# Three of the eight tiles of a depthwise convolution, computed in plain fp32 on 32x32 parts of the matmul array

## The chip, the cores and the metric

The kernel runs on one core of a Trainium2 chip. A core has a matmul engine (TensorE, PE in the profile; its weight loads are shown apart as PEld), a vector engine (DVE), a scalar engine (ACT), a general engine (POOL) and queues that issue DMA (SP and POOL here). The metric is the device time of one execution, in microseconds; shown is the median over runs.

## The reference, cut to what matters

The input is 512 positions of 1024 channels in fp32. There are two layers. The first has a state-space and attention mixer, the second a convolution module; each is followed by a layer norm, a square-relu MLP with 4096 hidden units, and another layer norm. The change lies in the convolution module of the second layer and in the addition that feeds its layer norms:

```python
def conformer_conv(x, w_pw1, b_pw1, w_dw, b_dw, ln_g, ln_b, w_pw2, b_pw2):
    h = x @ w_pw1 + b_pw1                       # 512 x 2048
    val, gate = jnp.split(h, 2, axis=-1)
    h = val * jax.nn.sigmoid(gate)              # 512 x 1024
    h = lax.conv_general_dilated(               # depthwise: 31 taps, each channel by itself
        h, w_dw[:, None, :], window_strides=(1,), padding=[(CONV_SIZE - 1, 0)],
        dimension_numbers=('NWC', 'WIO', 'NWC'), feature_group_count=CONV_WIDTH) + b_dw
    h = jax.nn.silu(layer_norm(h, ln_g, ln_b))
    return h @ w_pw2 + b_pw2

x = layer_norm(DEEPNORM_ALPHA * x + mix, ...)
x = layer_norm(DEEPNORM_ALPHA * x + sqrelu_mlp(x, ...), ...)
```

## The kernel before, in words

**Layout.** Activations are kept transposed: a tile is 128 channels by 512 positions, and 1024 channels are eight tiles (`KT`). A dense product is made in a split form: every fp32 operand is held as a high and a low half in a rounded fp32 format (fp32r), and each block of a product is three matmuls, high by high, high by low, low by high (`gemm`, whose matmuls carry L225). The weights of the conv module are split early in the program, kept in device memory, and fetched again by DMA from POOL's queue (L88).

**The convolution, tile by tile.** `glu_tile(j)` makes tile j's value `pv` and gate `pg` (24 matmuls each), takes a sigmoid on ACT (`csg`), multiplies on DVE (`hp`, fp32, with 30 zeros ahead for causality), and splits `hp` into `hph` (a cast on ACT, L215) and `hpl` (a subtraction on DVE, L216). The first two tiles' value and gate (`pl`) are made earlier, inside the layer norm ahead.

A depthwise tap scales each channel by its own weight. The kernel has two ways of doing it:
- `taps_pe`: ACT builds a 128x128 diagonal matrix with the tap's 128 weights, high part `dh` and low part `dl` (L154), and PE makes three matmuls with it into the accumulator `cv` (L1076). `DBUFS` is the number of buffers that these matrices rotate through.
- `taps_dve`: DVE makes one multiply-add over the tile for each tap (L357), in two running sums `cy` and `cz`. The first tap of each sum is made by ACT. At the end DVE adds `cy`, `cz` and `cv`.

`PE_TAPS` says how many of the 31 taps of each tile go to PE; the rest go to DVE, but for the two on ACT. The last two tiles (6 and 7) are worked in two halves of 256 positions: the first row of `PE_TAPS` holds for whole tiles and first halves, the second row for second halves. So PE makes 2+6+8+9+11+14 = 50 full-width taps and 13+14+13+8 = 48 half-width taps.

**What sets the order.** The code is written as a program, and the framework puts each engine's instructions into an order from the order in the program, the buffers and the data they need. Each engine then works through its own list in order. In the loop over the first six tiles, tile j+2's value and gate and tile j+1's PE taps are written ahead of tile j's DVE taps. `TAIL` is the written order for the halves of tiles 6 and 7: P for PE taps, V for DVE taps, G for the second half of the gate, N for the layer norm of one half. Then `tail_norm_lead` makes the second pointwise product (`tld`) and the next layer norm, with the first products of the MLP (`fl`) already begun. The two halves of that norm are reduced over channels by matmuls with a matrix of ones (L879: `mpc`, `vpc`), over sums `sc` that `LN.add` gathers tile by tile on DVE.

The matmul results rotate through PSUM: six banks of 128x512 fp32 for `pv`, `pg`, `cv` (`nps`), two for others (`stp`).

Of the kernel before, what the change touches and what calls it, by code (L numbers as in the profile page):

```python
# [9 lines left out]
F32 = mybir.dt.float32  # L10
# [155 lines left out]
def kernel(ctx: ExitStack, tc: tile.TileContext, a: dict, out: bass.AP):  # L166
# [47 lines left out]
    def split(hi, lo, src):  # L214
        i0 = S.copy(hi, src).ins  # L215
        i1 = V.tensor_sub(lo, src, hi.bitcast(F32)).ins  # L216
        return i0.name, i1.name
# [134 lines left out]
    def tt(o, x, y, op):  # L352
        V.tensor_tensor(o, x, y, op=op)  # L353
        return o
# [505 lines left out]
    class LN:  # L860
# [4 lines left out]

        def add(self, j, ys, c0, c1):

            if j == 1:
                self.s[c0] = tmp(f"s{self.n}{c0}")[:, c0:c1]
            if j:  # L870
                (V if j == KT - 1 or self.n in LN_ON_V else G).tensor_tensor(self.s[c0], ys[0][:, c0:c1] if j == 1 else self.s[c0], ys[j][:, c0:c1], op=ALU.add)

        def colmean(self, srcs, c0, c1, nm, other):

# [141 lines left out]
    wdh = hid.tile([P, KT, CONV], F32R, tag="wdh", name="wdh")  # L1016
    wdl = hid.tile([P, KT, CONV], F32, tag="wdl", name="wdl")

    def taps():
        for f in range(2):  # L1020
            wn = tmp(f"wn{f}")[:CONV]
            nc.sync.dma_start(wn, a["conv_w_dw"][0][:, f * T : (f + 1) * T])
            ps = stp(f"wd{f}")
            for i in range(4):
                PE.transpose(ps[:, i * 32 : i * 32 + CONV], wn[:, i * P : (i + 1) * P], ident[:CONV, :CONV])
            V.tensor_copy(wdw[:, 4 * f : 4 * f + 4, :], ps[:, :P].rearrange("p (i t) -> p i t", t=32)[:, :, :CONV])
        V.tensor_copy(wdh, wdw)
        V.tensor_sub(wdl, wdw, wdh.bitcast(F32))

    k0 = 0  # L1030
    for bi, nb in enumerate(FFN_BLOCKS[0]):
# [13 lines left out]
    def glu_tile(j, c0=0, c1=T):  # L1045
        if c0 == 0:
            if j < 2:
                ps[j] = first[2 * j : 2 * j + 2]
            else:
                ws[j], ps[j] = (W.next(), W.next()), (nps(f"pv{j}"), nps(f"pg{j}"))  # L1050
            hps[j] = hpage(f"hp{j}", F32, PAD + T), hpage(f"hph{j}", F32R, PAD + T), hpage(f"hpl{j}", F32R, PAD + T)
        vps, gps = ps[j]
        if j >= 2:
            gemm(vps, ws[j][0], slice(0, P), xs, c0, c1)
            gemm(gps, ws[j][1], slice(0, P), xs, c0, c1)
        sg = tmp(f"csg{j}{c0}")
        act(sg[:, c0:c1], gps[:, c0:c1], AF.Sigmoid, bias=pv("conv_b_pw1", 8 + j))
        hp, hh, hl = hps[j]
        p0 = PAD + c0 if c0 else 0
        if c0 == 0:  # L1060
            V.memset(hp[:, :PAD], 0.0)
        stt(hp[:, PAD + c0 : PAD + c1], vps[:, c0:c1], pv("conv_b_pw1", j), sg[:, c0:c1], ALU.add, ALU.mult)
        split(hh[:, p0 : PAD + c1], hl[:, p0 : PAD + c1], hp[:, p0 : PAD + c1])

    def taps_pe(j, c0=0, c1=T):
        _, hh, hl = hps[j]
        if c0 == 0:
            cps[j] = nps(f"cv{j}")
        n = PE_TAPS[c0 > 0][j]
# [5 lines left out]
            for i, (u, v) in enumerate(((dh, hh), (dh, hl), (dl, hh))):  # L1075
                PE.matmul(cps[j][:, c0:c1], u, v[:, t + c0 : t + c1], start=t == 0 and i == 0, stop=t == n - 1 and i == 2)  # L1076

    def taps_dve(j, c0=0, c1=T):

        hp = hps[j][0]  # L1080
        if c0 == 0:
            acc[j] = page(f"cy{j}", F32), hpage(f"cz{j}", F32)
        y, z = (x[:, c0:c1] for x in acc[j])
        t = CONV - 1
        act(y, hp[:, t + c0 : t + c1], AF.Identity, bias=pv("conv_b_dw", j), scale=wdw[:, j, t : t + 1])
        t = CONV - 2
        opened = act(z, hp[:, t + c0 : t + c1], AF.Copy, scale=wdw[:, j, t : t + 1])
# [3 lines left out]
        tt(y, y, z, ALU.add)  # L1091
        tt(y, y, cps[j][:, c0:c1], ALU.add)
        return opened

    ln = LN("c")
    n = KT - SPLIT_TILES
    cs_, ws, ps = None, [None] * KT, [None] * KT
    glu_tile(0)
    glu_tile(1)
    taps_pe(0)  # L1100
    for j in range(n):
        if j + 2 < KT:
            W.ahead = AHEAD[j + 2 >= n]
            glu_tile(j + 2, 0, T if j + 2 < n else H)
        if j + 1 < n:
            taps_pe(j + 1)
        opened = taps_dve(j)
        if j == 1:
            with tc.issue_after(opened):
                for i in range(KT):  # L1110
                    act(X[i], X[i], AF.Identity, bias=rb[2][:, i : i + 1], scale=ALPHA)
        for c0, c1 in HALVES:
            ln.add(j, [x and x[0] for x in acc], c0, c1)
    for o in TAIL:
        j, (c0, c1) = int(o[1]), HALVES[int(o[-1])]
        if o[0] == "P":
# [128 lines left out]
```

## Time and profile before

| What | Value |
|---|---|
| Time, median of 3 runs | 1219.02 us (1215.46 to 1219.36) |
| The profiled execution's own time | 1217.5 us |
| Its span in the trace | 1215.8 us |
| PE busy, share of the span | 1187.4 us, 98% |
| DVE busy | 786.9 us, 65% |
| ACT busy | 557.1 us, 46% |
| Mean clock granted to PE | 0.995 of full speed |

Times in the trace count from the span's start. The share of busy time is a mean over stages that differ, so a stage is read by a view that gives each engine's busy time in a stretch of the span. A PE matmul's end is modelled, so the time that a row of equal matmuls takes is read from start to start, or as the length of a stretch over their count. An fp32 matmul that is not in the fp32r format appears as two records.

### The profile page before, as it was taken

What the parts mean: (1) busy time and instruction counts of PE and PEld (TensorE: products, weight loads), DVE (VectorE), ACT (ScalarE), POOL (GpSimd) and SP (SyncE); (2) the same over time, 40 slices, a digit from 0 to 9 for tenths busy, and PEclk for the clock granted to TensorE, in tenths of its full rate; (3) what the DMA queues carried; (4) which work ended last, traced back from release to release, by engine and by line L of the source; (5) the groups of instructions that cost most, each with busy time, mean ns of one, the idle gap of its engine ahead of it and who ended that gap; (6) DMA issues with size and microseconds to landing.
All of it is one profiled execution on the core that took longest, in us unless ns stands there. A gap on an engine that the chain in (4) does not pass through costs nothing.

```text
span 1215.8 us, 16751 instructions
## 1 busy us (share of the span) xinstructions
PE 1187.4 (98%) x6546; PEld 1007.5 (83%) x6546; DVE 786.9 (65%) x1400; ACT 557.1 (46%) x990; POOL 58.2 (5%) x125
## 2 busy tenths in 40 slices
PE   9899999999999999999999999899999999999997
PEld 7677776789988888888999888889988888888885
DVE  7998774578745635646566999998843443434446
ACT  6836665734525524425323456964651332323230
POOL 1001101100000000000022110102000000000000
PEclk9999999999999999999999999999999999999999
DMA  8510042150878787887454631406142232323211
GB/s 205 155 49 22 19 130 61 31 195 1 264 250 282 251 284 264 270 283 268 165 183 159 213 104 36 139 1 208 39 152 87 87 108 83 122 70 121 70 52 69
DMA packets 128943, 168.86 MB, mean 139 GB/s; under 512 B 11298, under 2 KB 101666, under 8 KB 128864
## 3 DMA queue, kind: packets, MB, share of 16 engines
q1 hardware_dynamic: 120064, 136.30, 34.5%
q0 software_dynamic: 8640, 31.46, 7.6%
q8 instruction: 51, 0.84, 0.3%
q14 instruction: 28, 0.23, 0.1%
q10 hardware_dynamic: 160, 0.03, 0.0%
HBM read 132.12 MB, written 35.65 MB: 138 GB/s over the span
## 4 chain that ended last, share of the span: by engine, by line
PE 83%; DVE 10%; ACT 4%; DMA 2%; issue 1%; POOL 0%; SPq 0%; DVEq 0%; POOLq 0%; ACTq 0%
PE f L225 23%; PE g L1175 12%; PE acf L225 11%; PE fl L225 5%; PE tld L225 4%; PE tlb L225 4%; PE h L1159 3%; PE cv L1076 2%; PE pv L225 2%; PE pg L225 2%; PE tla L225 2%; PE pl L225 2%; DVE cz L357 1%; PE acmo L225 1%; PE av L709 1%
## 5 line engine op out<-in xcount | busy, mean ns | idle before, releaser
L102 DVE TENSOR_TENSOR wlo<-raw,whi 128x1024 fp32r<-128x1024 f32 x176 | 213.4, 1224 | 199.5 <-ACT whi L101 198.7
L101 ACT CAST whi<-raw 128x1024 fp32r<-128x1024 f32 x176 | 182.1, 1049 | 313.5 <-PE g L1175 107.4
L1175 PE MATMUL g<-whi,hh 128*128 128x512 f32 x208 | 81.8, 393 | 0.0
L1175 PE MATMUL g<-wlo,hh 128*128 128x512 f32 x208 | 81.8, 393 | 0.0
L1175 PE MATMUL g<-whi,hl 128*128 128x512 f32 x208 | 81.7, 393 | 0.0
L225 PE MATMUL f<-xah,whi 128*128 128x512 f32 x208 | 81.2, 390 | 0.0
L225 PE MATMUL f<-xdl,whi 128*128 128x512 f32 x208 | 81.1, 390 | 0.0
L225 PE MATMUL f<-xah,wlo 128*128 128x512 f32 x208 | 81.0, 390 | 0.0
L225 PE MATMUL f<-xdh,whi 128*128 128x512 f32 x208 | 81.0, 390 | 0.0
L225 PE MATMUL f<-xal,whi 128*128 128x512 f32 x208 | 81.0, 390 | 0.0
L225 PE MATMUL f<-xdh,wlo 128*128 128x512 f32 x208 | 81.0, 390 | 0.0
L225 PE MATMUL acf<-hl,whi 128*128 128x512 f32 x192 | 75.7, 394 | 0.0
L225 PE MATMUL acf<-hh,wlo 128*128 128x512 f32 x192 | 75.6, 394 | 0.0
L225 PE MATMUL acf<-hh,whi 128*128 128x512 f32 x192 | 75.5, 393 | 0.0
L215 ACT CAST hh<-fr 128x512 fp32r<-128x512 f32 x64 | 39.7, 621 | 59.6 <-DVE fr L353 59.6
L216 DVE TENSOR_TENSOR hl<-fr,hh 128x512 fp32r<-128x512 f32 x64 | 44.1, 690 | 31.9 <-ACT hh L215 31.8
L357 DVE SCALAR_TENSOR_TENSOR cy<-hp,wdw,cy 128x512 f32<-128x512 f32 (+1 forms) x99 | 63.6, 654 | 0.2
L357 DVE SCALAR_TENSOR_TENSOR cz<-hp,wdw,cz 128x512 f32<-128x512 f32 (+1 forms) x93 | 60.0, 656 | 0.0
L353 DVE TENSOR_TENSOR fr<-fr 128x512 f32<-128x512 f32 x64 | 43.7, 685 | 14.7 <-ACT fr L154 14.6
L1175 PEld LDWEIGHTS g<-wlo,hh 128*128 128x128 f32 x208 | 39.1, 188 | 8.9
L1175 PEld LDWEIGHTS g<-whi,hl 128*128 128x128 f32 x208 | 39.1, 188 | 8.9
L1175 PEld LDWEIGHTS g<-whi,hh 128*128 128x128 f32 x208 | 39.1, 188 | 8.8
(684 smaller groups left out, 3093.4 us busy)
## 6 DMA issues: line engine op xcount, KB each, us to landing
raw<-in_ffn_w_dram SPq DMA_DIRECT2D x48, 1024.0 KB, 5.8
raw<-in_ffn_w_dram SPq DMA_DIRECT2D x32, 512.0 KB, 3.5
kepth<-whi SPq DMA_DIRECT2D x30, 512.0 KB, 8.6
keptl<-wlo SPq DMA_DIRECT2D x30, 512.0 KB, 9.4
whi<-kepth POOLq DMA_DIRECT2D x30, 512.0 KB, 3.7
wlo<-keptl POOLq DMA_DIRECT2D x30, 512.0 KB, 4.5
raw<-in_conv_w_pw_dram SPq DMA_DIRECT2D x12, 1024.0 KB, 6.5
raw<-in_mix_w_in_dram SPq DMA_DIRECT2D x16, 512.0 KB, 3.9
```

What stands on the lines that cost most here:

```text
L101: i0 = nc.scalar.copy(hi, raw).ins
L102: i1 = nc.vector.tensor_sub(lo, raw, hi.bitcast(F32)).ins
L215: i0 = S.copy(hi, src).ins
L216: i1 = V.tensor_sub(lo, src, hi.bitcast(F32)).ins
L225: ins = PE.matmul(ps[:, c0:c1], u[:, k, ksl], v[:, c0:c1], start=start and k == 0 and i == 0, stop=stop and k == n - 1 and i == 2).ins
L353: V.tensor_tensor(o, x, y, op=op)
L357: V.scalar_tensor_tensor(o, x, s, y, op0=op0, op1=op1)
L709: ins = PE.matmul(av[R, P * kb :], vt[:, kb, R], ws_[f"{c}{h}"][0][:, o : o + T - P * kb], start=summed[h] == 1, stop=summed[h] == 4, skip ...
L1076: PE.matmul(cps[j][:, c0:c1], u, v[:, t + c0 : t + c1], start=t == 0 and i == 0, stop=t == n - 1 and i == 2)
L1159: PE.matmul(ps, u, v, start=k == 0 and i == 0, stop=k == nk - 1 and i == 2)
L1175: PE.matmul(pss[b], u, v[:, kk, :], start=k + kk == 0 and i == 0, stop=k + kk == nb - 1 and i == 2)
```

## The change

1. Tiles 2, 4 and 5 (`ON_PE`) have all 31 taps on PE, in plain fp32, by `taps_32`. The array is used as 16 parts of 32x32. Row part g works on channels 32g to 32g+31; the weights of tap t go to column part t modulo 4. One DVE operation builds the weights `D`: 31 blocks of 128x32, each a stack of four 32x32 diagonals. Each of the 31 taps then takes four matmuls (one per row part), 124 in all, each over 512 positions, into four PSUM banks `cw` (bank g for row part g). Within a bank, partitions 32c to 32c+31 hold the sum over the taps with t modulo 4 equal to c.
2. `merge` adds the four column parts: ACT copies each of the four banks to SBUF (`cq`), and one fp32 matmul each, with a stack of four identities (`mask`, 128x32), sums them into partitions 32g to 32g+31 of bank `cn`. `biased` moves that to SBUF with the bias, on ACT. These three tiles have no `hph`, `hpl`, no diagonals and no taps on DVE.
3. `PE_TAPS`: tiles 0 and 1 have all taps on DVE and ACT, tile 3 has 7 on PE, tile 6's halves 8 and 5, tile 7's 10 and 13. So the old form on PE falls to 7 full-width and 36 half-width taps.
4. `DBUFS` falls from 6 to 3. A tile's DVE taps are cut into three parts (`PARTS`), and a string `CONV_ORDER` gives the order: g for value and gate, p and m for the old and new PE taps, o for the merge, v for a third of the DVE taps, f for the bias of a merged tile, x for the scaling of the residual. `TAIL` begins with tile 7's first half.
5. `LN.add` starts its running sum with the first tile that is ready instead of with tile 0. The engine that does it is the same as before, DVE.

The order that the framework makes of it, at three places. First PE, after tile 2's value and gate (`pv`, `pg`), before:

```order
L225 MATMUL pg_6310<-xbh_5707,wlo_6252 128x512
L1076 MATMUL cv_6368<-hph_6266,dh_6369 128x512 [waits Activation_49]
L1076 MATMUL cv_6368<-hpl_6267,dh_6369 128x512 [waits DVE_49]
L1076 MATMUL cv_6368<-hph_6266,dl_6370 128x512
L1076 MATMUL cv_6368<-hph_6266,dh_6376 128x512
```

`hph_6266` is tile 1's: 18 such matmuls follow the gate of tile 2, on data that were made one tile earlier. And now, at the same place:

```order
L228 MATMUL pg_6299<-xbl_5712,whi_6255 128x512
L228 MATMUL pg_6299<-xbh_5711,wlo_6256 128x512
L1086 MATMUL cw_6378<-hp_6300,D_6376 32x512 [waits DVE_49]
L1086 MATMUL cw_6379<-hp_6300,D_6376 32x512
L1086 MATMUL cw_6380<-hp_6300,D_6376 32x512 [waits Activation_49]
L1086 MATMUL cw_6381<-hp_6300,D_6376 32x512
```

The matmuls after tile 2's gate now read `hp_6300`, which is tile 2's own and is made on DVE from that very gate. Second, PE at the end of the 124 matmuls, where the merge stands (now):

```order
L1086 MATMUL cw_6381<-hp_6300,D_6376 32x512
L228 MATMUL pv_6546<-xbh_5697,whi_6278 128x512 [waits DMASW4_49,Activation_49]
L228 MATMUL pv_6546<-xbl_5698,whi_6278 128x512
L228 MATMUL pv_6546<-xbh_5697,wlo_6279 128x512 [waits DMASW5_49]
L1095 MATMUL cn_6517<-cq_6518,mask 32x512 [waits Activation_49]
L1095 MATMUL cn_6517<-cq_6521,mask 32x512 [waits Activation_49]
L228 MATMUL pv_6546<-xbh_5699,whi_6278 128x512
L1095 MATMUL cn_6517<-cq_6524,mask 32x512 [waits Activation_49]
L228 MATMUL pv_6546<-xbl_5700,whi_6278 128x512
L228 MATMUL pv_6546<-xbh_5699,wlo_6279 128x512
L1095 MATMUL cn_6517<-cq_6527,mask 32x512 [waits Activation_49]
L228 MATMUL pv_6546<-xbh_5701,whi_6278 128x512
```

`pv_6546` is tile 3's value. The four merging matmuls stand among its matmuls in three places, each behind an ACT copy. The same pattern stands behind tile 4's 124 matmuls, in the value of tile 5. Behind tile 5's, six value matmuls of tile 6, three merging ones, four of tile 7 and the last merging one follow. Third, DVE, around the time when `hp` of tile 2 is made (now):

```order
L360 SCALAR_TENSOR_TENSOR cy_6353<-hp_6259,wdw,cy_6353 128x512 [waits DVE_49]
L360 SCALAR_TENSOR_TENSOR cz_6354<-hp_6259,wdw,cz_6354 128x512 [waits DVE_49]
L360 SCALAR_TENSOR_TENSOR hp_6300<-pv_6298,PV,csg_6349 128x512 [waits Activation_49]
L360 SCALAR_TENSOR_TENSOR cz_6354<-hp_6259,wdw,cz_6354 128x512 [waits DVE_49]
L360 SCALAR_TENSOR_TENSOR cy_6353<-hp_6259,wdw,cy_6353 128x512
```

`hp_6300` stands inside tile 0's chain of taps. `D_6376`, tile 2's weights, is built long before the convolution; `D_6747`, tile 4's, uses the same single buffer and stands later on DVE, waiting for the last of tile 2's 124 matmuls.

The diff, without the row of `LN.add` and of the tap loading that only follow from it:

```diff
-PE_TAPS = ((2, 6, 8, 9, 11, 14, 13, 14), (10, 10, 10, 10, 10, 10, 13, 8))
-TAIL = "P60 P70 V60 V70 G61 G71 N0 P71 P61 V61 V71 N1".split()
-DBUFS = 6
+PE_TAPS = ((0, 0, 0, 7, 0, 0, 8, 10), (10, 10, 10, 10, 10, 10, 5, 13))
+TAIL = "P70 P60 V60 V70 G61 G71 N0 P71 P61 V61 V71 N1".split()
+DBUFS = 3
+ON_PE = (2, 4, 5)
+PARTS = 3
+CONV_ORDER = "g0 g1 p0 g2 v0 p1 v0 m2 v0 o2 x0 g3 v1 f2 v1 g4 p3 m4 v3 v1 o4 g5 g6 m5 v3 o5 f4 v3 f5 g7".split()
...
-            hps[j] = hpage(f"hp{j}", F32, PAD + T), hpage(f"hph{j}", F32R, PAD + T), hpage(f"hpl{j}", F32R, PAD + T)
+            hps[j] = hpage(f"hp{j}", F32, PAD + T), *(() if j in ON_PE else (hpage(f"hp{x}{j}", F32R, PAD + T) for x in "hl"))
...
-        split(hh[:, p0 : PAD + c1], hl[:, p0 : PAD + c1], hp[:, p0 : PAD + c1])
+        if j not in ON_PE:
+            split(*(x[:, p0 : PAD + c1] for x in hps[j][1:] + (hp,)))
+
+    def taps_32(j):
+
+        D = hid.tile([P, CONV, 32], F32, tag="D", name=f"D{j}", bufs=1)
+        V.tensor_tensor(D, mask.unsqueeze(1).broadcast_to([P, CONV, 32]), wdw[:, j, :].unsqueeze(2).broadcast_to([P, CONV, 32]), op=ALU.mult)
+        cps[j] = [nps(f"cw{j}{g}") for g in range(4)]
+        for t in range(CONV):
+            for g in range(4):
+                R, C = slice(32 * g, 32 * g + 32), slice(32 * (t % 4), 32 * (t % 4) + 32)
+                PE.matmul(cps[j][g][C, :], D[R, t, :], hps[j][0][R, t : t + T], start=t < 4, stop=t >= CONV - 4,
+                          tile_position=(32 * g, 32 * (t % 4)))
+
+    def merge(j):
+
+        ps_ = stp(f"cn{j}")
+        for g in range(4):
+            q = tmp(f"cq{j}{g}")
+            S.copy(q, cps[j][g])
+            PE.matmul(ps_[32 * g : 32 * g + 32, :], mask, q, start=True, stop=True, tile_position=(0, 32 * g))
+        cps[j] = ps_
+
+    def biased(j):
+        acc[j] = page(f"cy{j}", F32), None
+        act(acc[j][0], cps[j], AF.Identity, bias=pv("conv_b_dw", j))
...
-        for i, t in enumerate(range(CONV - 3, PE_TAPS[c0 > 0][j] - 1, -1)):
+        n = PE_TAPS[c0 > 0][j]
+        todo = list(enumerate(range(CONV - 3, n - 1, -1)))
+        for i, t in todo[len(todo) * part // parts : len(todo) * (part + 1) // parts]:
...
-    for j in range(n):
...
+    for o in CONV_ORDER:
+        k, j = o[0], int(o[1])
+        if k == "g":
+            W.ahead = AHEAD[j >= n]
+            glu_tile(j, 0, T if j < n else H)
...
+        elif k != "p" or PE_TAPS[0][j]:
+            {"p": taps_pe, "m": taps_32, "o": merge}[k](j)
```

More of the change, by code (lines that the diff above doesn't have):

```diff
@@ L866, in add @@
         def add(self, j, ys, c0, c1):
[L868 to L871, printed above, removed]
+            y = ys[j][:, c0:c1]
+            if c0 not in self.s:
+                self.s[c0] = y
+            else:
+                if (c0, 0) not in self.s:
+                    self.s[c0, 0] = tmp(f"s{self.n}{c0}")[:, c0:c1]
+                tt(self.s[c0, 0], self.s[c0], y, ALU.add)
+                self.s[c0] = self.s[c0, 0]
         def colmean(self, srcs, c0, c1, nm, other):
@@ L1015 @@
     wdw = hid.tile([P, KT, CONV], F32, tag="wdw", name="wdw")
-    wdh = hid.tile([P, KT, CONV], F32R, tag="wdh", name="wdh")
-    wdl = hid.tile([P, KT, CONV], F32, tag="wdl", name="wdl")
+    most = max(PE_TAPS[0] + PE_TAPS[1])
+    wdh = hid.tile([P, KT, most], F32R, tag="wdh", name="wdh")
+    wdl = hid.tile([P, KT, most], F32, tag="wdl", name="wdl")
+    mask = hid.tile([P, 32], F32, tag="mask", name="mask")
     def taps():
@@ L1026, in taps @@
             V.tensor_copy(wdw[:, 4 * f : 4 * f + 4, :], ps[:, :P].rearrange("p (i t) -> p i t", t=32)[:, :, :CONV])
-        V.tensor_copy(wdh, wdw)
-        V.tensor_sub(wdl, wdw, wdh.bitcast(F32))
+        V.tensor_copy(wdh, wdw[:, :, :most])
+        V.tensor_sub(wdl, wdw[:, :, :most], wdh.bitcast(F32))
+        tt(mask, ident[:, :32], ident[:, 32:64], ALU.add)
+        tt(mask, mask, ident[:, 64:96], ALU.add)
+        tt(mask, mask, ident[:, 96:], ALU.add)
     k0 = 0
@@ L1057, in glu_tile @@
         act(sg[:, c0:c1], gps[:, c0:c1], AF.Sigmoid, bias=pv("conv_b_pw1", 8 + j))
-        hp, hh, hl = hps[j]
+        hp = hps[j][0]
         p0 = PAD + c0 if c0 else 0
@@ L1089, in taps_dve @@
             o = (y, z)[i % 2]
             stt(o, hp[:, t + c0 : t + c1], wdw[:, j, t : t + 1], o, ALU.mult, ALU.add)
-        tt(y, y, z, ALU.add)
-        tt(y, y, cps[j][:, c0:c1], ALU.add)
-        return opened
+        if part == parts - 1:
+            tt(y, y, z, ALU.add)
+            if n:
+                tt(y, y, cps[j][:, c0:c1], ALU.add)
     ln = LN("c")
     n = KT - SPLIT_TILES
[L1097 to L1100, printed above, removed]
-    for j in range(n):
[L1102 to L1109, printed above, removed]
+    cs_, ws, ps, last = None, [None] * KT, [None] * KT, {}
@@ L1110 @@
+    part = [0] * KT
+    for o in CONV_ORDER:
[3 more added lines that the diff above has]
+            glu_tile(j, 0, T if j < n else H)
+        elif k == "x":
+            with tc.issue_after(last["opened"]):
                 for i in range(KT):
                     act(X[i], X[i], AF.Identity, bias=rb[2][:, i : i + 1], scale=ALPHA)
-        for c0, c1 in HALVES:
-            ln.add(j, [x and x[0] for x in acc], c0, c1)
+        elif k in "vf":
+            if k == "f":
+                biased(j)
+            else:
+                part[j] += 1
+                taps_dve(j, 0, T, part[j] - 1, PARTS)
+                if part[j] < PARTS:
+                    continue
+            for c0, c1 in HALVES:
+                ln.add(j, [x and x[0] for x in acc], c0, c1)
+        elif k != "p" or PE_TAPS[0][j]:
+            {"p": taps_pe, "m": taps_32, "o": merge}[k](j)
```

15 lines of the change are left out of this document (8 added, 7 removed).

## The prediction, made before the changed kernel was timed

> **What bounds the kernel now.** I read the page first, then each stage of the convolution by engine, then the chain of waits.
>
> ```profile
> span 1215.8 us, 16751 instructions
> PE 1187.4 (98%) x6546; PEld 1007.5 (83%) x6546; DVE 786.9 (65%) x1400; ACT 557.1 (46%) x990; POOL 58.2 (5%) x125
> PE 83%; DVE 10%; ACT 4%; DMA 2%; issue 1%; POOL 0%; SPq 0%; DVEq 0%; POOLq 0%; ACTq 0%
> 628.00:667.07 39.07, 38.93 (x309) 38.15 (x308) 27.18 (x66) 14.45 (x30) 8.45 (x16) 1.00 0.56 189
> 667.07:757.13 90.06, 90.06 (x441) 75.83 (x440) 89.05 (x145) 50.11 (x131) 9.53 (x18) 1.00 0.37 126
> 757.13:778.76 21.63, 21.63 (x179) 21.32 (x177) 21.63 (x49) 19.20 (x61) 3.17 (x6) 1.00 0.36 118
> 778.76:795.48 16.72, 10.49 (x54) 9.03 (x55) 16.32 (x46) 14.88 (x39) 1.06 (x2) 0.90 0.29 100
> 795.48:848.70 53.22, 53.19 (x423) 52.36 (x424) 48.19 (x132) 29.29 (x71) 6.37 (x12) 1.00 0.35 118
> ```
>
> The lower rows are stretches of the span; behind the length stand the busy times of PE, PEld, DVE, ACT and POOL, then PE's granted clock. The changed code lies in 667 to 795 us. PE is busy in all of it but the fourth stretch, so time moves nearly one for one with PE's work there. DVE is as full as PE: 89.05 of 90.06 us in the second stretch. The one hole is 16.72 - 10.49 = 6.2 us in the fourth stretch, with a lower clock:
>
> ```profile
> PEld cv L1076 <- ACT hph L215: 4.2, 1, 4.2
> PEld cv L1076 <- ACT dh L154: 1.5, 1, 1.5
> 782.81 0.39 PE L1076 MATMUL cv<-hph,dh 128*128 128x256 f32 x1 [4.05 <-ACT hph L215]
> 783.96:789.03 5.07, 4.13 (x22) 3.86 (x23) 0.00 (x0) 0.74 0.01 2
> ```
>
> PE sits 4.05 us before the first tap of a second half; `hph` is late because its source `hp` stands on DVE behind a chain of taps. In the 5.07 us after it the clock is 0.74, which costs 0.26 x 5.07 = 1.3 us. Hole and clock together are about 7.5 us.
>
> **What is removed from PE.** Rows for the old matmuls (the first is from the chain: start, length, count; the second is a stretch of matmuls of 256 columns):
>
> ```profile
> 728.31 7.67 PE cv L1076 x33
> 629.68:641.28 11.60, 11.60 (x96) 11.53 (x96) 1.36 (x3) 1.00 0.94 313
> ```
>
> One full-width matmul takes 7.67/33 = 0.232 us, a half-width one 11.60/96 = 0.121 us. Full-width taps fall from 50 to 7: 43 x 3 x 0.232 = 29.9 us. Half-width ones fall from 48 to 36: 12 x 3 x 0.121 = 4.4 us. Removed: 34.3 us.
>
> **What is added on PE: the 124 matmuls.** The trace has no matmul on a 32x32 part. The nearest rows are plain fp32, whole array and column strips of 32:
>
> ```profile
> 650.50 1.74 PE vpb L879 x8
> 78.70:80.35 1.65, 1.64 (x62) 1.45 (x62) 0.00 (x0) 1.00 0.05 10
> 78.71 1.72 PE L528 MATMUL tp<-Cx,Gx 128*32 128x128 f32 x62
> 80.35 0.49 PE L542 MATMUL vI<-U,gt 128*128 128x128 f32 x2
> ```
>
> A plain fp32 record of 256 columns takes 1.74/8 = 0.2175 us, so one of 512 takes 0.435, and a product, which is two records, 0.87. The `tp` matmuls use strips of 32 columns of the array. 62 records of 128 columns end within 1.65 us. In one strip, 15.5 records of 128 columns would take 15.5 x 0.435/4 = 1.69 us by themselves, so the four strips run at the same time. It also bounds the issue from above: a record with its weight load needs no more than 1.65/62 = 27 ns. For row parts there are two rows of heads that use 64 rows each:
>
> ```profile
> 218.05 0.34 PE L672 MATMUL z3B<-ql,kh 64*128 64x384 f32 x1
> 218.23 0.33 PE L672 MATMUL z3B<-qh,kl 64*128 64x384 f32 x1
> 218.23 0.44 PE L672 MATMUL z3B<-qh,kh 64*128 64x384 f32 x2
> 218.46 0.38 PE L672 MATMUL z3B<-ql,kh 64*128 64x128 f32 x2
> ```
>
> A matmul of the second head (lower row half) starts in the same instant, 218.23, as one of the first head. So two row parts do run at once, and so do four column parts; that four by four do, no row shows. If all 16 run at once, the longest column part has 8 taps, and each row part takes its own: 8 x 0.87 = 7.0 us for a tile. The issue of 248 records takes 248 x 27 ns = 6.7 us at most, just under that. With a start of some 0.3 us, and a change of the array's partition at both ends, for which
>
> ```profile
> PEld vR L540 <- issue: 0.8, 4, 0.2
> ```
>
> gives 0.2 us (the switch from strips to the whole array), a tile costs 7.0 + 0.3 + 0.2 = 7.5 us. Lower bound 6.9 (nothing beside the matmuls), upper bound serial work, taken up under the rivals. I take 7.5, as the `tp` row has the same weights and the same strips. Three tiles: 22.5 us.
>
> **The merges.** Four plain fp32 matmuls of 0.87 us, each on its own strip of 32 columns, each behind an ACT copy of a bank. The nearest copy and the ACT and DVE steps that matter below:
>
> ```profile
> L1151 ACT COPY X<-xt 128x512 f32<-128x512 f32 x8 | 4.1, 620 | 0.0
> L160 ACT ACTIVATE csg<-pg,PV 128x512 f32<-128x512 f32 x4 | 2.7, 684 | 24.9 <-PE pg L225 24.9
> L357 DVE SCALAR_TENSOR_TENSOR hp<-pl,PV,csg x2: 747/750/752, 662.8 to 668.8; 128x512 f32<-128x512 f32 x2
> L357 DVE SCALAR_TENSOR_TENSOR cy<-hp,wdw,cy 128x512 f32<-128x512 f32 x64 | 46.5, 746 | 0.2
> L102 DVE TENSOR_TENSOR wlo<-raw,whi 128x1024 fp32r<-128x1024 f32 x176 | 213.4, 1224 | 199.5 <-ACT whi L101 198.7
> ```
>
> In PE's order a merge has three places: two products, one, one. The first two overlap, so three turns of 0.87 = 2.6 us; three visits to the strips with 0.2 us for the way in and out make 0.6. Three value matmuls stand ahead of the first, 0.7 us, and the first copy needs 0.62 and a signal: a wait of about 0.4 in all. That is 3.6 us a merge, 10.8 for three. From below: all four products at once, and one visit, 0.87 + 0.2 = 1.1 a merge, 3.2 in all; not likely, since the order has full-array matmuls between them. From above: each copy waited for alone, 4 x (0.62 + 0.87) + 6 x 0.2 = 7.2 a merge, 21.5 in all.
>
> **Waits that are added and removed.** The first of tile 2's 124 now reads tile 2's own `hp`. Behind the last `pg` come the sigmoid (0.68), then up to one tap of 0.66 that DVE is in, then `hp` (0.75), which PE must sit through: 0.68 + 0.75 + half a tap, and signals, about 1.9 us; bounds 1.4 and 2.3. Queued behind it on PE is the value of tile 3, for which nobody waits at that moment, but PE is the bound, so it counts. Tile 4's has the 21 old tap matmuls of tile 3 between (21 x 0.232 = 4.9 us) and tile 5's the half gate of tile 6 (48 x 0.121 = 5.8 us), so these two waits are covered. `D` (like the 128x1024 row, 1.2 us) is built by DVE well ahead.
>
> ```profile
> 757.38 0.66 DVE cy L357
> L357 DVE SCALAR_TENSOR_TENSOR cy<-hp,wdw,cy 128x256 f32<-128x256 f32 x35 | 17.1, 488 | 0.0
> 667.92 0.39 ACT L154 ACTIVATE dh<-ident,wdh 128x128 fp32r<-128x128 f32 x1
> 668.21 0.39 ACT L154 ACTIVATE dl<-ident,wdl 128x128 fp32r<-128x128 f32 x1
> 668.50 0.39 ACT L154 ACTIVATE dh<-ident,wdh 128x128 fp32r<-128x128 f32 x1
> ```
>
> DVE loses 124 - 80 = 44 full taps at 0.66 us (its step in the chain), gains 80 - 68 = 12 half ones at 0.49, three builds of `D`, and loses three subtractions for `hpl`: about 21 us less. ACT loses 55 pairs of diagonals and gets 12 copies and three bias moves. That takes pressure off `hp` of the second halves. It does not take the taps away that stand ahead of it: the halves have more DVE taps than before, 80 for 68. I let a third of the 7.5 us go, 2.5 us; bounds 0 and 7.5. `DBUFS` of 3 I cost at nothing: 15 or 18 half taps stand together instead of 21, ACT makes a pair in about 0.6 us (from 667.92 to 668.50) against 0.36 us of PE for a half tap, so ACT is behind within a run whatever the depth, and deeper buffers only store a lead of three pairs, at most 3 x 0.6 = 1.8 us for a run; that is inside the bounds of this term. `LN.add` moves no engine's work.
>
> **The sum**: -34.3 + 22.5 + 10.8 + 1.9 - 2.5 = -1.6 us. Against the profiled execution (span 1215.8, own time 1217.5) that is 1215.9; the median of the runs shown is 1.5 above that execution, so the prediction is 1217.4 us. The own range of this case: merges 2.5 less or 5 more for all three, the wait term between 0 and 5, together 1213 to 1222. What a measurement of this kernel can tell from no change is about 0.3%, 3.7 us, so "the same" is 1215.4 to 1222.7.
>
> [...] The rows `tp` and `z3B` show records that run beside each other. [...]
>
> **Rivals.**
>
> 1. *More is gained.* With DVE 21 us lighter the second halves' `hp` comes in time, and the hole and the slow clock after it go altogether: 5.0 us beyond the 2.5. For it: the hole is the only stretch in which PE idles, and it is DVE's queue that makes it. Against it: the half taps on DVE grow. -1.6 - 5.0 = -6.6, that is 1212.4.
>
> 2. *Fewer row parts at once (the side of slower).* The rows show two row parts at once, not four, and none where row and column parts are both cut. If two of the four run at a time, the 124 matmuls take 14.0 us instead of 7.0: 3 x 7.0 = +21.0 us, and the sum is +19.4: 1238.4. It decides from where the sum passes +3.7 us, 5.3 us above mine: when a tile's 124 take over 7.5 + 5.3/3 = 9.3 us. For it: no row speaks for four. Against it: nothing in the `z3B` rows shows two as a limit.
>
> 3. *Strict order.* Each product's second record waits for its first: 124 x 0.435 = 54 us a tile instead of 7.0, +141 us in three: 1358. Speaking against it: `tp`, where the same order would have cost 62 x 0.109 = 6.8 us and took 1.65.
>
> 4. *The merges cost their upper bound.* Copies are waited for one by one, since only three and one full-array matmuls (0.7 and 0.23 us) cover a copy of 0.62: 21.5 instead of 10.8, the sum is +9.1: 1228. For it: these covers are thin. Against it: ACT can make all four copies in a row.
>
> **Chances.** My forecast 0.50, more gained 0.20, fewer row parts 0.15, dear merges 0.10, strict order 0.05. Faster by over 0.3% (below 1215.4): 0.15 of the forecast's half and 0.18 of the first rival, 0.33. Within: 0.32, and 0.02 each of the first and the fourth, 0.36. Slower: 0.03, 0.08, 0.15 and 0.05, 0.31. The range is 1209 to 1240: it leaves out strict order, the upper part of the second rival and the lowest of the first.
>
> **What would show it.** In the changed profile the `cw` group: 248 records in about 7.0 us for a tile, from its first start to the next `pv`; 14 us would show two row parts, 54 strict order. The three `cn` visits of a merge: 3.6 us beyond the value matmuls between them. An idle entry of about 1.9 us before the first `cw`, put down to DVE's `hp`, and none before those of tiles 4 and 5. The stretch of the old hole: an idle time before a second half's first `cv` of 2 to 4 us, with a clock below 1. In the removed part, `cv` groups of 21 and 108 records at the same 0.232 and 0.121 us. The prediction fails if the overlap is partial, or if DVE, not PE, sets the end of the convolution.

## The result, and the profile after

The changed kernel takes 1221.86 us (median of 10 runs), the kernel before 1217.65 us (median of 10). The ratio is 1.0028, 95% interval 1.0017 to 1.0040: about 3.4 us slower (2.1 to 4.9 by the interval; the two medians lie 4.2 apart), where 1.6 us faster was forecast. The time lies inside the range that was given, but on the other side of the kernel before. The profiled execution has a span of 1219.3 us, 3.5 us more than the one before.

The page of the changed kernel, its first two rows:

```profile
span 1219.3 us, 17760 instructions
PE 1192.0 (98%) x7149; PEld 996.0 (82%) x7149; DVE 761.8 (62%) x1363; ACT 526.2 (43%) x886; POOL 58.2 (5%) x125
```

DVE has lost 25 us and ACT 31, and PE has 5 us more to do. The stretches of the convolution (length, then busy time of PE, PEld, DVE, ACT, POOL, then PE's clock):

```profile
679.56:718.86 39.30, 39.30 (x373) 27.27 (x374) 34.61 (x56) 10.70 (x24) 4.21 (x8) 1.00 0.40 132
718.86:748.12 29.26, 29.26 (x353) 20.19 (x353) 17.80 (x30) 4.06 (x8) 2.11 (x4) 1.00 0.22 73
748.12:768.10 19.98, 19.98 (x324) 13.73 (x323) 6.90 (x17) 5.01 (x11) 0.00 (x0) 1.00 0.01 2
768.10:784.01 15.91, 15.85 (x132) 15.83 (x132) 15.85 (x41) 13.65 (x44) 3.16 (x6) 1.00 0.49 158
784.01:797.72 13.71, 9.16 (x42) 6.91 (x40) 12.34 (x35) 12.52 (x32) 1.05 (x2) 0.88 0.36 125
```

PE is full until 784. DVE, full before, is now busy for 17.8 of 29.3 us from 719 to 748 and for 6.9 of 20.0 to 768, and then as full as before in the halves of tiles 6 and 7. The hole is still there (the last row). The chain of waits (start, length, count) shows what PE does in between; `cw` are the small matmuls, `cn` the merging ones:

```profile
679.56 8.62 PE cw L1086 x229
688.18 0.89 PE pv L228 x3
689.08 1.26 PE cn L1095 x4
690.34 0.43 PE pv L228
690.77 0.97 PE cn L1095 x2
691.74 0.67 PE pv L228 x2
692.41 0.97 PE cn L1095 x2
693.38 4.31 PE pv L228 x18
697.69 5.44 PE pg L228 x24
...
714.02 4.91 PE cv L1113 x21
718.93 8.55 PE cw L1086 x228
727.48 0.90 PE pv L228 x3
...
737.00 5.44 PE pg L228 x24
...
748.19 8.55 PE cw L1086 x228
```

A tile's small matmuls take 8.55 us, not 7.5. From the first value matmul after them (688.18) to the next gate (697.69) lie 9.5 us; 24 value matmuls alone take 5.44, so the merge adds 4.1 us; the second one the same (727.48 to 737.00). The third stands among half-width matmuls and adds 3.3 us, read in the same way. The waits of PE's weight loads (total, times, longest):

```profile
PEld cv L1113 <- ACT hph L218: 2.5, 2, 2.2
PEld cw L1086 <- DVE hp L360: 2.2, 1, 2.2
PEld cv L1113 <- ACT dl L157: 1.4, 1, 1.4
PEld cv L1113 <- ACT dh L157: 0.8, 1, 0.8
```

The account against the prediction's sum, in us of PE time:

| Term | Predicted | In the two traces |
|---|---|---|
| old matmuls removed | -34.3 | -34.3 (the rows' prices hold: 21 full-width in 4.91) |
| 372 small matmuls (three tiles) | +22.5 | 3 x 8.55 = +25.7 |
| merges | +10.8 | 4.1 + 4.1 + 3.3 = +11.5 |
| wait ahead of tile 2's | +1.9 | +1.9 |
| hole at the end | -2.5 | -1.4 |
| sum | -1.6 | +3.4 |

The hole is the stretch from the last gate to the second pointwise product: 16.7 us before, of which 44 half-width matmuls of taps and the reductions are 7.1; 13.7 us now, of which 29 such matmuls and the reductions are 5.3. PE loses 9.6 before and 8.4 after, some 0.2 us of the difference lying in where the stretch is cut. So two terms were off: the small matmuls by 3.2 us and the hole by 1.1; the merges add another 0.7.

### The profile page after: what moved, and what is told of

It is laid out like the page before. It is cut to its first block, busy times and chain, and to the rows that moved or that the text cites. A ratio compares the mean times of both kernels' runs of the same rounds, so it can differ in the third digit from the quotient of the medians.

```text
span 1219.3 us, 17760 instructions
## 1 busy us (share of the span) xinstructions
PE 1192.0 (98%) x7149; PEld 996.0 (82%) x7149; DVE 761.8 (62%) x1363; ACT 526.2 (43%) x886; POOL 58.2 (5%) x125
## 4 chain that ended last, share of the span: by engine, by line
PE 79%; DVE 10%; ACT 4%; DMA 4%; issue 2%; SPq 1%; POOL 0%; DVEq 0%; ACTq 0%; POOLq 0%
PE f L228 20%; PE g L1222 12%; PE acf L228 10%; PE fl L228 5%; PE tld L228 4%; PE tlb L228 3%; DMA raw<-in_ffn_w_dram 3%; PE h L1206 3%; PE pv L228 2%; PE cw L1086 2%; PE pg L228 2%; DVE wlo L105 2%; PE cv L1113 1%; ACT whi L104 1%; PE acmo L228 1%
## 5 line engine op out<-in xcount | busy, mean ns | idle before, releaser
L360 DVE SCALAR_TENSOR_TENSOR cy<-hp,wdw,cy 128x512 f32<-128x512 f32 (+1 forms) x82 | 50.5, 616 | 0.8
L360 DVE SCALAR_TENSOR_TENSOR cz<-hp,wdw,cz 128x512 f32<-128x512 f32 (+1 forms) x78 | 46.1, 615 | 0.0
```

What stands on the lines that cost most here:

```text
L360: V.scalar_tensor_tensor(o, x, s, y, op0=op0, op1=op1)
```

## The experiments

All ratios are to the kernel before, with 95% intervals.

### Why the small matmuls take 8.55 us: their order

Sixteen parts with eight products of two records of 0.43 us each would be done 7.0 us after the start. The timeline of the weight loads in the changed kernel (start, length, count, idle time ahead):

```profile
679.56 0.24 PEld L1086 LDWEIGHTS cw<-hp,D 32*32 32x32 f32 x32 [2.18 <-DVE hp L360]
680.01 0.10 PEld L1086 LDWEIGHTS cw<-hp,D 32*32 32x32 f32 x1 [0.21 <-issue]
680.44 0.55 PEld L1086 LDWEIGHTS cw<-hp,D 32*32 32x32 f32 x32 [0.32 <-issue]
```

32 loads go at once: first and second record of 16 products, so all 16 parts do work at a time, and the four-by-four overlap that no row of before showed is there (248 records of 0.43 us in 8.55 us are 12 to 13 at a time). But when the second records start, at 680.01, only one load for the next product goes ahead. The next group begins only at 680.44, when the parts are free again. A product is four instructions in the trace, two loads and two matmuls. Times 16 parts, that makes 64 instructions from one product of a part to the next; the look-ahead of about 64 instructions in e2's expectation is this count, an estimate. Four runs asked whether it is this distance.

**e1 and e2: other orders of the same matmuls.** e1 puts the row part outermost, e2 the column part:

```diff
-        for t in range(CONV):
-            for g in range(4):
+        for g in range(4):            # e1
+            for t in range(CONV):
...
-        for t in range(CONV):
+        for t in sorted(range(CONV), key=lambda t: t % 4):      # e2, g inside
```

> The 124 small matmuls of a tile in another order: all 31 taps of row part 0, then of row part 1, and so on (the column part still goes with the tap modulo 4). In the changed kernel they take 8.55 us a tile; a round of one product in each of the 16 parts takes 1.07 us where the two records alone take 0.86, and the weight load of a round's products starts only just before their matmuls. Theory A (a look-ahead of limited length over the program's order: the queue sees about one round of 16 products, so the next product's weights come too late): in this order the look-ahead holds only four column parts of one row part, so about four parts work at a time and a tile takes 124 x 0.87 / 4 = 27 us, the kernel +55 us. Theory B (every part, or every column strip, is fed by itself and the loss is at the product's boundary): 8.5 us, no change. Theory C (a bound on issue, 248 records at 34.5 ns): 8.5 us, no change.

> The same 124 matmuls with the column part outermost: the eight taps of column part 0 over the four row parts, then column part 1, and so on; this is the order of the strips in the tp rows, which did run beside each other. Theory A (look-ahead of about 64 instructions): four row parts at a time, 27 us a tile, +55 us. Theory B (each strip is fed by itself, as the tp rows suggest): a part's next product is four products away instead of sixteen, its weights come in time, and a tile takes 7.0 to 7.5 us, -3 to -4.5 us in all. Theory C (issue): 8.5 us.

e2, the chain and the weight loads:

```profile
680.42 21.82 PE cw L1086 x248
...
680.42 0.15 PEld L1086 LDWEIGHTS cw<-hp,D 32*32 32x32 f32 x8 [2.17 <-DVE hp L360]
680.87 0.12 PEld L1086 LDWEIGHTS cw<-hp,D 32*32 32x32 f32 x4 [0.30 <-issue]
681.30 0.12 PEld L1086 LDWEIGHTS cw<-hp,D 32*32 32x32 f32 x4 [0.30 <-issue]
681.73 0.12 PEld L1086 LDWEIGHTS cw<-hp,D 32*32 32x32 f32 x4 [0.30 <-issue]
```

Four parts work at a time, one load each every 0.43 us, without a gap. A tile takes 21.8 us (one run, 1260.83 us). It is less than the 27 of four parts throughout, so the next strip must have begun before the last one's end. In e1 a tile takes 40 to 43 us (1320.47 us), more than any theory had; its stretches of small matmuls show why in the clock, the first number behind the busy times:

```profile
681.50:723.00 41.50, 41.50 (x238) 9.43 (x231) 16.94 (x26) 1.76 (x3) 0.00 (x0) 0.50 0.02 7
752.56:791.80 39.24, 39.24 (x246) 9.45 (x248) 14.60 (x24) 2.38 (x5) 0.00 (x0) 0.55 0.00 1
```

At a clock of 0.50 to 0.55 these are 21 to 22 us of full clock, e2's time. Theory A, a look-ahead of limited length, holds; B and C said 7.0 to 8.5.

**e3: each small matmul in two halves of 256 positions.**

```diff
+        for c0, c1 in HALVES:
             for t in range(CONV):
                 for g in range(4):
-                PE.matmul(cps[j][g][C, :], D[R, t, :], hps[j][0][R, t : t + T], ...
+                    PE.matmul(cps[j][g][C, c0:c1], D[R, t, :], hps[j][0][R, t + c0 : t + c1], ...
```

> Each of the 124 matmuls is cut into two of 256 positions, first all 124 for the first half, then all for the second: the same work in twice as many instructions. Theory C (issue bound, 34.5 ns a record): 496 records take 17.1 us a tile, +25.7 us in all. Theory A or B (a fixed loss of about 0.22 us at each round's boundary, else the array's own time): a round takes 2 x 0.2135 + 0.22 = 0.65 us, 15.5 rounds 10.0 us a tile, +4.4 us in all.

The stretches of the first two tiles:

```profile
681.26:692.68 11.42, 10.56 (x496) 7.35 (x496) 11.42 (x19) 0.00 (x0) 0.00 (x0) 1.00 0.25 89
723.41:735.77 12.36, 10.59 (x498) 7.39 (x497) 12.36 (x21) 0.62 (x2) 0.00 (x0) 1.00 0.02 5
```

A tile takes 11.4 to 12.5 us (1234.56 us, one run), where a bound on issue wanted 17.1 and a fixed loss at each round 10.0. In the steady part a round of 16 products is 0.65 us, as worked out; the rest are two or three pauses in a tile, 0.9 to 1.8 us in all, whose cause no view shows. So issue is not the bound: 496 records take 11.4 us where 34.5 ns each would make 17.1. Nor is it a limit on how much 16 parts can do at once, since the 0.22 us lost in a round stay the same when the work of a round is halved.

**e9: three column parts, tap modulo 3.** The distance falls to 12 products, 48 instructions. The start and stop flags follow; the copies take 96 partitions, and POOL writes zeros into the rest.

```diff
-                R, C = slice(32 * g, 32 * g + 32), slice(32 * (t % 4), 32 * (t % 4) + 32)
+                R, C = slice(32 * g, 32 * g + 32), slice(32 * (t % 3), 32 * (t % 3) + 32)
```

> The changed kernel with three column parts in use instead of four (tap modulo 3), so 12 parts of the array; the merge reads 96 partitions, the other 32 are zeros. The result is the same sum. A part's next product stands 12 products away in the program instead of 16. The two ends for a tile: a loss of 0.22 us at every round whatever the distance gives 10.3 rounds of 1.07, 11.1 us and more; a look-ahead that holds about 12 products but not 16 gives rounds of 0.86 with no loss, 8.9 to 9.3 us. With the look-ahead, the fourth column part is worth almost nothing in this order (8.55 against 9 us).

```profile
681.14 9.68 PE cw L1086 x233
...
681.13 0.21 PEld L1086 LDWEIGHTS cw<-hp,D 32*32 32x32 f32 x24 [2.18 <-DVE hp L360]
681.59 0.14 PEld L1086 LDWEIGHTS cw<-hp,D 32*32 32x32 f32 x5 [0.24 <-issue]
```

The deepest column part has 11 taps, 22 records of 0.43 us: 9.5 us, and 0.15 for the last one's end. It took 9.68: nothing is lost (one run, 1224.74 us; the expectation had counted 10.3 rounds for 11). Five loads of the next round go ahead here, at 681.59, where the changed kernel has one, at 680.01: 12 products and five loads, or 16 products and one, both reach as far as the 17th product. Four of the five belong to the column part with 11 taps. The other seven products of that round start some 0.2 us late, once, in column parts with 10 taps, which have 0.86 us to spare. With four column parts the same count gives 7.0, and 8.62 were taken. The fourth column part is worth 1.1 us a tile instead of 2.6. In the first round of both kernels the loads go ahead as far as 16 products of four instructions and one load more. No run changes the distance and leaves the number of parts as it is, so that it is the distance rests on these loads and on e1 to e3. A product's two records do not stand together in time: in the changed kernel 16 first records start within 0.11 us, from 679.56 to 679.67, all of them before the second record of the first product, at 680.01. Product by product, the order may still hold; the trace does not number its products.

### What the merges and the entry waits are worth

**e4: the merging matmuls together, behind the next tile's gate.** The copies stay, the four matmuls get a letter of their own in the order:

```diff
+    def copied(j):
+        cqs[j] = [...]                        # the four ACT copies
-CONV_ORDER = "... m2 v0 o2 x0 g3 v1 f2 v1 g4 p3 m4 v3 v1 o4 g5 g6 m5 v3 o5 f4 v3 f5 g7"
+CONV_ORDER = "... m2 v0 c2 x0 g3 o2 v1 f2 v1 g4 p3 m4 v3 v1 c4 g5 o4 g6 m5 v3 c5 f4 v3 g7 o5 f5"
```

> The copies stay where they are, but the four merging matmuls of a tile stand together behind the whole next value and gate, with their copies long done, instead of in three places among the next value's matmuls. In the changed kernel a merge adds 4.0, 4.0 and 3.2 us to PE. Theory D (the cost is the three visits to the column strips and the copies waited for): one visit with four products at once, 0.87 + 0.4 = about 1.3 us each, -7 us in all, ratio to the kernel before about 0.997. Rival (four products on four strips do not overlap, 4 x 0.87): 3.5 us each, within 1 us of the changed kernel, ratio 1.002 to 1.003.

```profile
695.04 5.44 PE pg L228 x24
700.48 0.99 PE cn L1102 x8
701.48 5.67 PE pv L228 x24
```

Four products on four strips take 1.0 us, not 3.5, so they overlap, and the matmuls beside them lose some 0.2. A merge falls from 4.1 to 1.2 us, as theory D said. The edit takes away two things, the visits and the copies waited for. In the changed kernel these waits make only 1.4 us in all three merges (`cn` for `cq`), so the visits are the larger part. The kernel comes to 0.9998 (0.9986 to 1.0009), 3.6 us under the changed one; of the 8 us won in the merges the hole took 3.7 back. It is 17.4 us long instead of 13.7: PE waits 3.3 us there for the second halves' `hph`, where it was 2.2, and its clock is 0.71, where it was 0.88.

**e5 to e8: three edits over e4, alone and together.** e5 moves tile 3's seven taps to DVE (`PE_TAPS[0][3] = 0`), e6 puts the small matmuls of tiles 4 and 5 later, e7 puts tile 3's value and gate ahead of tile 2's small matmuls, e8 does all three.

> The kernel with late merges, and tile 3's seven taps go from PE (21 matmuls) to DVE, so that no full-width tap is left in the old form. In the kernel with late merges DVE stands idle for 5.65, 4.2 and 13.8 us between 731 and 760 us, while PE is full. Theory E (the freed time of DVE lies idle in the middle of the convolution, PE is the bound there): 21 x 0.232 = 4.9 us less, seven DVE taps fit into the idle time; ratio to the kernel before about 0.996. Rival (DVE is as full as before where it counts, so its taps delay what follows): no gain or a loss, ratio 0.999 or more.

> The kernel with late merges, and the small matmuls of tiles 4 and 5 stand later: tile 4's behind the value and gate of tile 5, tile 5's behind the first half of tile 7's. In the kernel with late merges PE loses about 12 us between the end of the second halves' gate (777.8) and the second pointwise product (795.2), behind a DVE that has the halves' taps to do from 762 on and was idle before. Theory E (the stall at the end is DVE starting the halves too late): the halves' values come 17 us of PE work earlier, PE does the small matmuls while DVE works, and 5 to 8 us of the 12 go; ratio about 0.994 to 0.996. Rival (the stall comes from the layer norm of the halves itself): same as the kernel with late merges, 0.9998.

> The kernel with late merges, and the value and gate of tile 3 stand ahead of tile 2's small matmuls, so that these no longer wait for data that were made just before. The changed kernel waits 1.76 us there. Theory F (that wait lies on the path): it goes, 1.8 us less, ratio about 0.998. Rival (the time comes back as a longer stall at the end of the convolution): ratio 1.000.

> The three edits of the runs beside this one together, over late merges: tile 3's taps on DVE, the small matmuls of tiles 4 and 5 later, tile 3's value ahead of tile 2's. If each is worth what theories E and F say: 4.9 + 6 + 1.8 = 12.7 us below the kernel with late merges, ratio to the kernel before about 0.989. If the stall at the end only moves: 0.996 or more.

| Run | Ratio | Where it went |
|---|---|---|
| e5 | 0.9996 (0.9987 to 1.0006) | the waits for `hp` ahead of small matmuls go from 2.2 us in one place to 5.1 in two: tile 3's taps had covered tile 4's |
| e6 | 1.0075 (1.0063 to 1.0087) | tile 5's small matmuls are split by six others: 7.0 and 7.4 us, not 8.55 together |
| e7 | 1.0038 (1.0026 to 1.0050) | the wait leaves tile 2's and stands ahead of tile 4's, 4.1 us |
| e8 | 1.0024 (1.0013 to 1.0035) | as e6 |

None of the three is worth what the row of its work says. The waits of e5, e7 and e6, in this order:

```profile
PEld cw L1087 <- DVE hp L360: 5.1, 2, 2.9
...
PEld cw L1087 <- DVE hp L360: 4.1, 1, 4.1
...
PEld cw L1087 <- issue: 9.3, 33, 0.3
PEld mpc L886 <- DVE sc L356: 3.8, 1, 3.8
```

The longer waits cost more than their length, since the clock granted behind them is lower. Tile 4's small matmuls in e7 (0.73) and in e5 (0.83):

```profile
716.97:728.29 11.32, 11.32 (x249) 6.44 (x249) 10.83 (x17) 0.01 (x1) 0.00 (x0) 0.73 0.01 3
...
713.12:723.25 10.13, 10.13 (x249) 5.95 (x249) 10.13 (x19) 0.00 (x0) 0.00 (x0) 0.83 0.20 72
```

Behind waits of 4.1 and 2.9 us they take 11.3 and 10.1 us at a mean clock of 0.73 and 0.83; behind the 2.2 us ahead of tile 2's in the changed kernel it was 8.6 at 1.00. With that the sums come out: e5 wins 4.9 and loses 2.9 + 1.6 us, e7 wins 1.9 and loses 4.1 + 2.8.

In e6 the framework put 62 of tile 5's small matmuls, six of a value, and the other 62; the loads stand idle 33 times instead of 9 in e4, and the layer norm's first reduction waits 3.8 us for DVE. The likely reason for the split is that the values of tiles 6 and 7 hold four of the six PSUM banks; that was argued, not tried.

### The hole at the end: ACT's list, latency, DVE's start

**e12: the changed kernel with the old order of the halves; e13: that, with the openings first.** Two edits of one line, and in e13 the two ACT operations that open a half's sums on DVE get a letter A of their own:

```diff
-TAIL = "P70 P60 V60 V70 G61 G71 N0 P71 P61 V61 V71 N1"
+TAIL = "P60 P70 V60 V70 G61 G71 N0 P71 P61 V61 V71 N1"                      # e12
+TAIL = "A60 A70 P60 P70 V60 V70 G61 G71 N0 A61 A71 P71 P61 V61 V71 N1"      # e13
```

> The changed kernel with the halves of tiles 6 and 7 in the order of the kernel before (tile 6's first half first). If the new order is worth something at the end of the convolution, PE's loss between the second gate and the second pointwise product (13.7 us of which 5.3 are work, before the change 16.9 and 7.1) grows by 1 us or more; ratio 1.004. Rival (the loss is set by DVE's chain, whatever the order of the two tiles on PE): the same as the changed kernel, 1.003.

> The run with the old order of the halves, and the two ACT operations that open a half's two running sums on DVE stand in the program ahead of the halves' PE taps, whose 18 pairs of diagonals ACT builds. In the run with the old order DVE waited 7.75 us for the second opening, behind these pairs. Theory G (that queue on ACT is what the order of the halves costs): 7 to 8 us go, ratio to the kernel before 1.003 to 1.005. Rival (the order of the two tiles on PE costs by itself): 1.009 to 1.011.

e12 is at 1.0107 (1.0089 to 1.0125), 13 us over the kernel before and nearly 10 over the changed one. One wait of DVE explains most of it:

```profile
DVE cz L360 <- ACT cz L157: 7.7, 1, 7.7
```

ACT works through 15 of the 18 pairs of diagonals for PE's taps, from 767.4 to 776.5, and the opening of `cz`, for which DVE's whole list waits, stands behind them. In e13 the row is gone and the ratio is 1.0026 (1.0013 to 1.0040). So the two letters that the change swapped in `TAIL` carry nearly 10 us, through ACT's list.

**e10, e11, e14, e15: towards a faster kernel.** e10 is e5 with the gate's matmuls ahead of the value's, so that the sigmoid runs beside the value. e11 adds the order that covers both entry waits, e14 the openings first, e15 DVE's taps of tile 6's first half right behind tile 5's small matmuls:

```diff
-            gemm(vps, ws[j][0], slice(0, P), xs, c0, c1)
             gemm(gps, ws[j][1], slice(0, P), xs, c0, c1)
+            gemm(vps, ws[j][0], slice(0, P), xs, c0, c1)
...
-CONV_ORDER = "... m2 v0 c2 x0 g3 o2 v1 f2 v1 g4 p3 m4 v3 v1 c4 g5 o4 g6 m5 v3 c5 f4 v3 g7 o5 f5"
+CONV_ORDER = "... g3 m2 v0 c2 x0 g4 o2 v1 f2 v1 v3 v1 g5 m4 v3 c4 g6 o4 f4 m5 v3 c5 g7 o5 f5"           # e11, e14
+CONV_ORDER = "... g3 m2 v0 c2 x0 g4 o2 v1 f2 v1 v3 v1 g5 m4 v3 c4 g6 o4 f4 m5 v3 a6 u6 c5 g7 o5 f5"     # e15
```

> The kernel with late merges and tile 3's taps on DVE, and in each tile the gate's 24 matmuls stand ahead of the value's, so that the sigmoid on ACT runs while the value is made. In the run before it PE waited 2.14 us ahead of tile 2's small matmuls and 2.87 ahead of tile 4's for gate, sigmoid, product; the sigmoid is about 0.7 of each. Theory F (these waits are chains of latency: gate, sigmoid, product on DVE): 0.7 less at each of the two and 0.4 to 0.7 at the second halves, about 2 us, ratio to the kernel before 0.998. Rival (the product waits for its turn on DVE, so an earlier sigmoid changes nothing): 0.9996.

> The kernel of the run beside this one (late merges, tile 3 on DVE, gate first), and each tile's small matmuls stand behind the next tile's gate and value: tile 2's behind tile 3's, tile 4's behind tile 5's. Theory F: the two entry waits are covered, 1.4 and 2.2 us less than beside, and the next wait does not come since no tile follows its own data; ratio 0.995 to 0.996. Rival (what was won at the entry returns as a longer stall before the second halves, as when tile 3's value alone stood ahead): as the run beside, 0.998.

> The fastest kernel so far (late merges, tile 3 on DVE, gate first, small matmuls behind the next tile), and the openings of the halves' sums on ACT stand ahead of the halves' PE taps. In that kernel DVE waits 3.3 us for an opening, and PE then 7.4 us for the second halves' hph. Theory G: 3.3 us less, ratio to the kernel before 0.995. Rival (DVE's chain has slack there): 0.998.

> The same kernel, and DVE's 20 taps of tile 6's first half stand right behind tile 5's small matmuls instead of behind tile 7's value. In the fastest kernel so far DVE is idle for 13.1 us just before. Theory E (the stall at the end is DVE starting the halves too late, with its idle time ahead): 20 x 0.4 = 8 us of DVE's work move into the idle time, PE's wait of 7.4 us for hph goes down to 1 or less, ratio 0.992 to 0.993. Rival (hph is late by its own chain of gate, sigmoid and product): the wait stays over 3 us, ratio 0.995 or more.

| Run | Ratio | PE's longest wait for the second halves' `hph` |
|---|---|---|
| e10 | 1.0013 (1.0000 to 1.0026) | 7.6 us |
| e11 | 0.9979 (0.9969 to 0.9988) | 7.6 us |
| e14 | 0.9941 (0.9926 to 0.9956) | 2.8 us |
| e15 | 0.9900 (0.9886 to 0.9915) | 1.1 us |

e10 missed: the entry waits did fall, but the framework's new order put a part of the diagonals ahead of an opening again, DVE waited 3.3 us for it, and the hole grew. e11 covers the entries; e14 takes the opening out of ACT's queue, and its gain of 4.6 us is at least theory G's 3.3; e15 moves DVE's work into its idle time, and the wait goes down to 1.1 us, about what theory E said. e15 takes 1204.28 us, 1.0% less than the kernel before. Its last two stretches, up to the second pointwise product:

```profile
752.70:769.90 17.20, 17.20 (x145) 17.17 (x145) 15.65 (x40) 15.47 (x45) 3.16 (x6) 1.00 0.45 143
769.90:781.46 11.56, 7.45 (x42) 5.68 (x40) 11.13 (x32) 10.71 (x30) 1.05 (x2) 1.00 0.45 152
```

The hole's stretch is 11.6 us instead of 13.7, the clock stays at 1.00, and the product starts at 781.5 instead of 797.7. Of these 16.2 us, 14.1 lie ahead of the hole: the late merges, tile 3's matmuls, the entry waits. The hole itself is only 2.1 us shorter; what the last two edits do is that it does not take the rest back, as in e10 and e11, where it is 20.2 us long.

**e16 and e17: two of these edits, and one, in the changed kernel.** e16 has the openings first and tile 6's DVE taps early (the last edit of e15), e17 the gate first.

> The changed kernel itself with only that: the openings ahead of the halves' PE taps, and DVE's taps of tile 6's first half right behind tile 5's small matmuls. In the changed kernel DVE waits 11.6 us for ACT's bias move of tile 5 and 7.2 us for a sigmoid while PE is full, and PE loses 8.4 us at the end. Theory E: about half of these 8.4 us go, ratio to the kernel before 0.999 to 1.000. Rival: no change, 1.003.

> The changed kernel with one edit: the gate's matmuls ahead of the value's. Theory H (what is left of the stalls in the changed kernel is latency from gate over sigmoid, product and cast back to PE: 2.14 us at tile 2's small matmuls and 2.23 at the second halves): the sigmoid's 0.7 and 0.5 us go from the two, about 1.2 us less, ratio to the kernel before 1.002. Rival (the order of ACT and DVE that the framework then makes costs more than the latency saves, as in the run with gate first over late merges): 1.004 or more.

e16 is at 1.0037 (1.0024 to 1.0051), no better than the changed kernel: theory E falls there. DVE started earlier, and PE still waited for `hph`, 2.3 us. In e17 the two waits on this chain shrink,

```profile
PEld cw L1086 <- DVE hp L360: 1.5, 1, 1.5
...
PEld cv L1113 <- ACT hph L218: 1.4, 2, 1.2
```

from 2.2 to 1.5 and from 2.2 to 1.2 us, and the ratio is 1.0019 (1.0008 to 1.0030). The interval overlaps that of the changed kernel, so the gain of about 1 us is shown by the waits rather than by the time. The second pointwise product starts 2.9 us earlier, at 794.85, but its stretch takes 2.8 us longer, at a mean clock of 0.96 instead of 1.00; why, was not looked into. In the changed kernel the wait in the hole is latency, gate to sigmoid to product to cast, and not DVE's queue.

**e18: the orders without the small matmuls.** The kernel before with the gate first and the openings first.

> The kernel before, without any 32x32 part, with two of the edits of the fastest kernel that can be made in it: the gate's matmuls ahead of the value's, and the openings of the halves' sums on ACT ahead of the halves' PE taps. If the gain of the fastest kernel (ratio 0.990) comes from these orders alone, this kernel comes to 0.992 or less. If it needs the small matmuls, which free DVE and PE for the orders to use, DVE stays full here (89 of 90 us busy) and the ratio is 0.997 to 1.001.

0.9992 (0.9983 to 1.0002), with PE's wait for `hph` at 4.0 us, as before. So these two orders alone gain nothing in the kernel without the small matmuls. The likely reason is that DVE is full there (89.05 of 90.06 us busy from 667 to 757), and an earlier start of its lists has nowhere to go; that is argued from its busy time.

## Why the prediction was wrong, point by point

- **What bounds the kernel, and the removed work**: right. PE is full up to the hole, and 21 full-width matmuls take 4.91 us in the changed kernel, 0.234 each.
- **The 124 small matmuls, 7.5 us a tile**: this is the step that failed, by 3 x 1.05 = 3.2 us. The mechanism, 16 parts at once, was right, and issue was not the bound (e3). The term had no width in the prediction's own range, which let only the merges and the waits vary. Of the 0.5 us added to 7.0, the 0.3 for a start stood on no row, and no run shows it: in e9, where nothing is lost between the rounds, 22 records of 0.43 us make 9.5 us and the tile took 9.68. What was missing is that a part's next weights come too late when its next product stands 64 instructions away (the timeline of the loads, e2, e9). I took the `tp` rows as proof that order does not matter, with one strip's records standing in the program before the next strip's. That was misread: in the program each strip gets two products and then the next one has its turn, so these rows never tested a long distance. Nor do they all have 128 columns, as I took it: the four strips have 128, 96, 64 and 32. The first strip's 16 records alone fill the 1.7 us, so that the strips run beside each other stands, but one after the other they would take about 4.4 us, not 6.8 (an estimate from the same 0.109 us).
- **The merges, 3.6 us**: 3.8 in the mean. The three visits and the copies waited for were the cost, as e4 showed (1.0 us in one visit, with the copies done).
- **The wait of 1.9 us ahead of tile 2's**: right, in place, size and cause; e17 shows the sigmoid's share.
- **The hole, -2.5 us**: -1.4. The sign was right, by luck. The guess of a third stood on DVE's relief; the relief came where DVE had nothing to hurry for (6.9 of 19.98 us busy from 748 to 768), and the wait in the hole was latency (e16, e17). What decided there was the order on ACT, which the prediction did not cost: the sum has no term for the new `TAIL`, and e12 shows nearly 10 us for its two letters. With the old ones the hole is 19.8 us long, where it was 16.7 before, although DVE has the same relief.
- **DBUFS at nothing**: not tried by itself, so it stays open.
- **The rivals**: fewer row parts and strict order did not happen (32 loads and 16 matmuls at once, 8.55 us a tile and not 14 or 54); the merges stayed near their middle; more gained came true only with other orders (e15).
- **The chances**: with the two mis-sized terms the sum, with the merges' 0.7, is +3.4 us, at the edge between "the same" and "slower"; the range held the time.

## What to carry to other kernels

Before packing small matmuls on parts of the array, count the instructions from one product on a part to the next: 16 (e2) and 48 (e9) cost nothing here, 64 cost a fifth of the time. The order must also keep all parts in reach: the same work took 8.55 us in turn over all parts and 21.8 with one column part after the other. When a change frees an engine, look at where its idle time falls; in these runs it was worth something only where the order of work let that engine start earlier what was late at the end, and each in-order list on the way (ACT's was worth 10 us) has to be read. An edit that is worth its microseconds by the rows can come back as a wait at the next place that lost its cover, as in e5 and e7, where the clock behind the longer waits was 0.83 and 0.73.

## What the runs showed of the hardware that was not expected

With four column parts of a single row part at work, PE's granted clock fell to 0.50 to 0.55 and stayed there for 39 to 41 us (e1). With four row parts of a single column part it stayed at 1.00 for 21.7 us (e2):

```profile
680.42:702.16 21.74, 21.74 (x248) 6.56 (x248) 18.59 (x28) 0.00 (x0) 0.00 (x0) 1.00 0.13 46
```

Both have four parts busy and the same work, so the number of busy parts alone does not set the clock. What does was not looked into further.
